# Four small filler tiles that move the split operands of the matmuls to the start of a 128-byte line of SBUF

## The chip, the cores and the metric

One core of a Trainium2 chip runs the whole program. The metric is the device time of one execution in microseconds (us). TensorE (PE in the profile) multiplies, ScalarE (ACT), VectorE (DVE) and GpSimd (POOL) do the rest, and SyncE (SP) issues the DMAs.

## The reference

The input is 256 tokens of 1024 features. It goes through two layers of a first block (here: layers A) and two of a second (layers B), all in float32. A layer is a mixer (projections, linear or gated recurrences, attention), a gated feed-forward network with 2816 hidden features, and a gate that adds a projected side input. The core of it:

```
u = rms_norm(h, g);  parts = split(u @ w_in);  ... mixers ...
h = h + (mixed @ w_out)                         # A: with a norm after it
g, u = split(rms_norm(h) @ w_ffn_in);  h = h + (silu(g) * u) @ w_ffn_out
h = h + gate(h @ w_ple_gate) * (p @ w_ple_proj)
```

A layer B has a second feed-forward network ahead of its mixer.

## The kernel before, in words

**Every product is three matmuls.** A float32 operand x is split into xh, its rounding to the type float32r that TensorE reads in one pass, and xl, what the rounding leaves. The product is xh·wh + xl·wh + xh·wl. The weights come as tiles of [128, 1024] float32 (512 KB): `weight` (lines 219 to 243) lets SP fetch one into `raw` (4 buffers), ScalarE writes `hi` (L241) and VectorE `lo` (L242), five buffers each. SP fetches ahead, as far as buffers are free, and ACT and DVE split ahead of TensorE.

**Two loops use them.** `gemm_fm` (lines 263 to 285) has the weights as the stationary operand, a block of 128×128 each, and lets 256 columns of the split input stream by (L279 to L281): 24 matmuls to a weight tile. `gemm_tm` (lines 287 to 317) has a block of the split input stationary and streams 512 columns of `hi` or `lo` (L306 to L308): 12 matmuls to a weight tile. In the trace, "acc<-xTh,hi" at L279 is a matmul that streams xTh against the stationary hi, and "acc<-hi,xTh" at L306 one that streams hi against the stationary xTh. TensorE loads the next stationary block while the matmul ahead of it streams.

**The split inputs** are the pairs xTh/xTl (normed input of every projection, pool `act`), hh/hl (hidden features of the network), oh/ol, yh/yl and mh/ml (inside the mixers), xrh/xrl (input of layer A's last gate, class `Raw`) and px (the side input).

**Where tiles lie.** A pool takes a stretch of bytes of each of the 128 partitions, and pools and tiles are laid one behind the other in the order in which the code makes them, each tile in a whole number of 32 bytes. The order is `const`, `wraw`, `whl`, `act`, `small` (lines 185 to 193), then `tmp` (temporaries), `hT` in layers B, and a pool of each mixer or network. The scheduler orders the instructions by priorities and a simulated timeline, and knows nothing of where a tile lies within a line.

The first pool, `const`, starts on a multiple of 128 bytes and holds ident (512 bytes), h (8192), expo (64) and ones (512): 9280 bytes, which is 72 lines of 128 and 64 over. So `raw`, `hi` and `lo` (4096 each) and xTh, xTl (8192 each) begin 64 bytes into a line. What a tile's first byte is past the start of a 128-byte line, called its phase here, is by the same addition:

| tiles | phase before | phase after |
|---|---|---|
| raw, hi, lo, xTh, xTl | 64 | 0 |
| hh, hl, xrh, xrl of layers A | 96 | 0 |
| hh, hl of layers B | 0 | 0 |
| oh, ol, mh, ml of layers A | 0 | 0 |
| oh, ol, yh, yl, mh, ml, left, right of layers B | 96 | 0 |
| px made in layers A / in layers B | 96 / 0 | 96 / 0 |
| ra, up (the matmuls "z", L821) | 0 | 0 |
| ident, h | 0 | 64 |
| temporaries t of layers A / layers B | 96 / 0 | 96 / 0 |

The slices that matmuls read start 512, 1024 or 2048 bytes apart, so that a slice has the phase of its tile. The third column is the same addition with the fillers of the change. [...]

Of the kernel before, what the change touches and what calls it, by code (L numbers as in the profile page):

```python
# [11 lines left out]
F32 = mybir.dt.float32  # L12
# [6 lines left out]
P = 128  # L19
# [19 lines left out]
HOLD_LAST = (1, 3)  # L39
HOLD_B = 4  # L40
LAG = 3


class Norm:
# [3 lines left out]
    def __init__(self, net, g, tag="xT"):  # L48
        self.net, self.g = net, g
        self.xs = net.pair(net.act, tag)  # L50
        self.r = [None, None]
        self.R = net.act.tile([P, S], F32, tag="R", name=net.name("R"), bufs=2)
        self.ssq = [net.small.tile([P, 2], F32, tag="nssq", name=net.name("nssq")) for _ in range(2)]
# [124 lines left out]
class Net:  # L178
    def __init__(self, ctx, tc, a, raw_bufs=4, w_bufs=5, acc_bufs=3):
        self.tc = tc  # L180
        self.nc = tc.nc
        self.a = a
        pool = lambda name, bufs, **kw: ctx.enter_context(tc.tile_pool(name=name, bufs=bufs, **kw))
        psum = bass.MemoryType.PSUM
        self.const = pool("const", 1)
        self.wraw = pool("wraw", raw_bufs)
        self.whl = pool("whl", w_bufs)
        self.act = pool("act", 1)
        self.small = pool("small", 4)
        self.ps = pool("ps", acc_bufs, space=psum)  # L190
        self.pt = pool("pt", 2, space=psum)
        self.pm = pool("pm", 2, space=psum)
        self.pg = pool("pg", 1, space=psum)
        self.n = 0


        self.hold = self.held = None
        self.fetched = []
        nc = self.nc
        self.ident = self.const.tile([P, P], F32, name="ident")  # L200
        self.h = self.const.tile([P, 2, D], F32, name="h")
        self.expo = self.const.tile([P, 16], F32, name="expo")
        nc.vector.memset(self.expo, -0.5)
        self.ones = self.const.tile([P, P], F32, name="ones")
        nc.vector.memset(self.ones, 1.0)

    def temporaries(self, ctx, bufs):
        self.tmp = ctx.enter_context(self.tc.tile_pool(name=self.name("tmp"), bufs=1))
        self.tmp_bufs = bufs
# [164 lines left out]
    def ffn(self, nrm, wi, wo, epi, pool, fm=False):  # L374
# [21 lines left out]
        else:  # L396
            self.gemm_tm((hh, hl), wo, epi, lag=LAG)

# [110 lines left out]
def layer_a(net, i, nrm, following):  # L509
    nc, a, tc = net.nc, net.a, net.tc  # L510
    with ExitStack() as mx:
        nrm, px = mixer_a(net, i, mx, nrm)
    with tc.tile_pool(name=net.name("ffn"), bufs=1) as fp:
        g_post = net.gain(a["g_ffn_post"][i])
        e = ple_proj(net, px, a["w_ple_proj"][i])
        raw = Raw(net, fp)
        net.ffn(nrm, a["w_ffn_in"][i], a["w_ffn_out"][i], net.post_norm(g_post, raw, fp, HOLD_FFN), fp)
        g_post = net.gain(a["g_ple_post"][i])
        nrm = following()
        px = ple_input(net, a["pT_2"][0]) if i + 1 == DEPTH else None  # L520

        def gated(tt, hf, acc):
            cs = slice(hf * 512, (hf + 1) * 512)
            t = net.t()
            nc.scalar.activation(t, acc, AF.Sigmoid)
            nc.vector.tensor_tensor(t, t, e[:, tt, cs], ALU.mult)
            return t

        net.gemm_tm(raw.xs, a["w_ple_gate"][i], net.post_norm(g_post, nrm, fp, HOLD_PLE if i + 1 < DEPTH else HOLD_LAST, gated), lag=LAG)
    return nrm, px  # L530


def ple_input(net, pT):
    with net.urgent(SPLIT_PRIO, 200):
        raw = net.t()
        net.nc.sync.dma_start(out=raw, in_=pT)
        px = (net.t((P, 2, S), F32R, "px"), net.t((P, 2, S), F32R, "px"))
        net.split_fm(raw, *px, 0)
    return px


def ple_proj(net, px, w):
    nc = net.nc
    e = net.t((P, 2, D), tag="e")
    net.gemm_tm(px, w, lambda tt, hf, acc: nc.scalar.copy(e[:, tt, hf * 512:(hf + 1) * 512], acc))
    return e
# [98 lines left out]
def mixer_a(net, i, cx, nrm):  # L645
# [40 lines left out]
    def rope_heads(tt, acc, nh, w, dst, h0):  # L686
        n = nh * P
        x = net.t()[:, :n]
        nc.scalar.activation(x, acc, AF.Copy, scale=r[tt])
        return lambda: rope_rest(tt, x, nh, w, dst, h0)  # L690
# [21 lines left out]

    net.gemm_tm(xs, a["w_aq"][i], lambda tt, hf, acc: rope_heads(tt, acc, 4, 0, q_t, hf * 4), lag=LAG if i else 0)
    if i == 0:
# [92 lines left out]
    px = ple_input(net, a["pT"][i])  # L807
    net.gemm_tm(ms, a["w_out"][i], net.post_norm(g_post, nrm, p1, HOLD_MIX, tags={"hg": "gg", "xg": "b1", "yg": "b0"}), lag=LAG)
    return nrm, px
# [84 lines left out]
def layer_b(net, i, nrm, px, hT, following):  # L894
# [12 lines left out]
    with ExitStack() as cx:  # L907
        ms = mixer_b(net, i, cx, after)
        px = ple_input(net, a["pT_2"][i])
        nrm = NormT(net, hT, col(2))  # L910
        net.gemm_fm(ms, a["w_o"][i], net.add_scaled(hT, 1.0, nrm.blocks), tail=True)
# [20 lines left out]
def mixer_b(net, i, cx, nrm):  # L932
    nc, a, tc = net.nc, net.a, net.tc
    p1 = cx.enter_context(tc.tile_pool(name=net.name("mx"), bufs=1))
    big = lambda tag, dt=F32: p1.tile([P, KB, S], dt, tag=tag, name=net.name(tag))
    fl = lambda t: t.rearrange("p a b -> p (a b)")
    xs, rs = nrm.xs, nrm.r
# [143 lines left out]
def _build(tc, a, out):  # L1081
    with ExitStack() as ctx:
        net = Net(ctx, tc, a)
        nc = tc.nc
        with ExitStack() as part:
            net.temporaries(part, T_BUFS_A)
            net.split = SPLIT_A
            nrm = lambda pool: first_norm(net, pool)
            nxt = [lambda: Norm(net, net.gain(a["g_mix_pre"][1])), lambda: Norm(net, net.gain(a["ffn1_norm_2"][0]))]
            for i in range(DEPTH):  # L1090
                nrm, px = layer_a(net, i, nrm, nxt[i])

        hp = ctx.enter_context(tc.tile_pool(name="hT", bufs=1))
        net.hp = hp
        net.temporaries(ctx, T_BUFS_B)
        net.split = SPLIT_B
        hT = hp.tile([P, KB, S], F32, name="hT")
        for tt in range(2):
            for hf in range(2):
                ps = net.pt.tile([P, 4, P], F32, tag="pt", name=net.name("pt"))  # L1100
                for j in range(4):
                    kb = hf * 4 + j
                    nc.tensor.transpose(ps[:, j], net.h[:, tt, kb * P:(kb + 1) * P], net.ident)
                nc.scalar.copy(hT[:, hf * 4:hf * 4 + 4, tt * P:(tt + 1) * P], ps)
        gc = hp.tile([P, 16], F32, name="gc")
        nc.sync.dma_start(out=gc, in_=a["gains_last"])
        nxt = [lambda: NormT(net, hT, gc[:, 0:8]), lambda: NormT(net, hT, gc[:, 8:16], out)]
        for i in range(DEPTH):
            nrm, px = layer_b(net, i, nrm, px, hT, nxt[i])
# [140 lines left out]
```

## Time and profile before

| | us |
|---|---|
| median of 3 runs | 2347.22 (2344.7 to 2348.76) |
| the profiled execution | 2343.83 |
| its span, first to last instruction | 2342.1 |
| TensorE busy in the span | 2292.5 |
| VectorE busy | 1602.7 |
| ScalarE busy | 1333.8 |
| mean share of the 16 DMA engines | 56% |

A matmul's busy time in the profile runs from its start to a modelled end, some 280 ns for 256 columns, and consecutive ones overlap. What a stream of matmuls costs is the distance between their starts. It is read from the first and the last start of a run and the count between: x instructions of one line, each followed by one of the two other lines of its loop, are 3(x-1) distances.

### The profile page before, as it was taken

The page shows a single profiled execution, that of the slowest core. Times are in us where ns is not written, and L with a number is a line of the kernel's source. Part 1 is how long each engine was busy: PE and PEld are TensorE (multiplying, and loading weights), DVE is VectorE, ACT ScalarE, POOL GpSimd, SP SyncE. Part 2 cuts the span into 40 slices and gives each one's busy share as a digit, 9 for nine tenths or more (in the row PEclk, how much of TensorE's full clock was granted, in tenths as well). Part 3 has the DMA queues.
Part 4 walks back from the last instruction along what each step waited for, and adds up shares of the span by engine and source line. Part 5 has one row for each costly group of instructions (what it writes and reads, how often), then busy time and mean ns, then how long its engine had stood idle before and what let it go on. Part 6 is the DMA issues. An engine that isn't in the chain of part 4 may idle for free.

```text
span 2342.1 us, 42188 instructions
## 1 busy us (share of the span) xinstructions
PE 2292.5 (98%) x16892; PEld 2176.4 (93%) x16892; DVE 1602.7 (68%) x2133; ACT 1333.8 (57%) x2105; POOL 441.0 (19%) x443
## 2 busy tenths in 40 slices
PE   8999999998999999999999999999999999999997
PEld 6899899878899998799999899999999998999997
DVE  7876766487867765665586867665755677766555
ACT  6874554467864644554456765444644557755444
POOL 5222111054302110211001302110111103012101
PEclk9999999999999999999999999999999999999999
DMA  7445566544455665546656555556556665456563
GB/s 253 145 153 162 186 196 182 180 167 146 146 162 176 203 184 183 174 163 182 190 182 189 161 152 183 184 186 197 172 181 188 188 188 168 149 169 190 181 190 99
DMA packets 117102, 411.53 MB, mean 176 GB/s; under 512 B 14114, under 2 KB 16546, under 8 KB 116906
## 3 DMA queue, kind: packets, MB, share of 16 engines
q1 hardware_dynamic: 116906, 408.84, 55.9%
q8 instruction: 133, 2.18, 0.4%
q14 instruction: 63, 0.52, 0.1%
HBM read 407.74 MB, written 1.05 MB: 175 GB/s over the span
## 4 chain that ended last, share of the span: by engine, by line
PE 89%; DVE 4%; POOL 3%; issue 2%; ACT 1%; DMA 1%; SPq 0%; DVEq 0%; POOLq 0%; ACTq 0%
PE acc L280 22%; PE acc L279 22%; PE acc L281 22%; PE acc L306 5%; PE acc L307 5%; PE acc L308 5%; DVE lo L242 1%; POOL t L703 1%; PE sc L572 1%; PE po L583 1%; PE gs L880 1%; ACT hi L241 1%; PE sc L596 0%; POOL hg L72 0%; DMA gq<-g_q_norm 0%
## 5 line engine op out<-in xcount | busy, mean ns | idle before, releaser
L242 DVE TENSOR_TENSOR lo<-raw,hi 128x512 fp32r<-128x512 f32 (+1 forms) x1062 | 985.5, 954 | 435.8 <-ACT hi L241 430.8
L241 ACT ACTIVATE hi<-raw 128x512 fp32r<-128x512 f32 (+1 forms) x1062 | 824.2, 808 | 764.5 <-PE acc L280 399.1
L279 PE MATMUL acc<-xTh,hi 128*128 128x256 f32 x3296 | 936.3, 284 | 8.8 <-ACT t L1049 7.2
L280 PE MATMUL acc<-xTl,hi 128*128 128x256 f32 x3296 | 938.8, 285 | 0.7 <-DVE xTl L127 0.5
L281 PE MATMUL acc<-xTh,lo 128*128 128x256 f32 x3296 | 936.5, 284 | 0.0
L279 PEld LDWEIGHTS acc<-xTh,hi 128*128 128x128 f32 x3296 | 634.4, 193 | 10.9 <-ACT t L1049 7.6
L280 PEld LDWEIGHTS acc<-xTl,hi 128*128 128x128 f32 x3296 | 634.6, 193 | 2.6 <-DVE xTl L127 1.5
L281 PEld LDWEIGHTS acc<-xTh,lo 128*128 128x128 f32 x3296 | 634.5, 193 | 0.4
L387 POOL TENSOR_TENSOR t<-t,R 128x512 f32<-128x512 f32 x66 | 105.8, 1603 | 624.6 <-ACT t L385 624.6
L279 PE MATMUL acc<-hh,hi 128*128 128x256 f32 x704 | 194.3, 276 | 0.0
L280 PE MATMUL acc<-hl,hi 128*128 128x256 f32 x704 | 194.3, 276 | 0.0
L281 PE MATMUL acc<-hh,lo 128*128 128x256 f32 x704 | 194.3, 276 | 0.0
L306 PE MATMUL acc<-hi,xTh 128*128 128x512 f32 x416 | 163.5, 398 | 6.5 <-ACT hi L241 6.5
L307 PE MATMUL acc<-lo,xTh 128*128 128x512 f32 x416 | 165.2, 397 | 1.4 <-DVE lo L242 1.3
L308 PE MATMUL acc<-hi,xTl 128*128 128x512 f32 x416 | 163.9, 395 | 0.1
L279 PEld LDWEIGHTS acc<-hh,hi 128*128 128x128 f32 x704 | 132.2, 188 | 0.0
L280 PEld LDWEIGHTS acc<-hl,hi 128*128 128x128 f32 x704 | 132.2, 188 | 0.0
L281 PEld LDWEIGHTS acc<-hh,lo 128*128 128x128 f32 x704 | 132.2, 188 | 0.0
L306 PEld LDWEIGHTS acc<-hi,xTh 128*128 128x128 f32 x416 | 78.7, 190 | 22.0 <-ACT hi L241 6.5
L307 PEld LDWEIGHTS acc<-lo,xTh 128*128 128x128 f32 x416 | 78.9, 190 | 17.9 <-DVE lo L242 2.7
L308 PEld LDWEIGHTS acc<-hi,xTl 128*128 128x128 f32 x416 | 78.7, 189 | 16.7 <-DVE xTl L342 0.8
L370 DVE TENSOR_TENSOR t<-acc,R 128x512 f32<-128x512 f32 (+1 forms) x84 | 56.9, 677 | 47.3 <-PE acc L281 46.3
(321 smaller groups left out, 3235.7 us busy)
## 6 DMA issues: line engine op xcount, KB each, us to landing
raw<-ffn_w_in SPq DMA_DIRECT2D x176, 512.0 KB, 3.7
raw<-w_ffn_in SPq DMA_DIRECT2D x88, 512.0 KB, 3.8
raw<-ffn_w_out SPq DMA_DIRECT2D x88, 512.0 KB, 3.6
raw<-w_ffn_out SPq DMA_DIRECT2D x44, 512.0 KB, 4.0
raw<-w_gate SPq DMA_DIRECT2D x32, 512.0 KB, 3.8
raw<-w_gab SPq DMA_DIRECT2D x32, 512.0 KB, 3.6
raw<-w_gqk SPq DMA_DIRECT2D x16, 512.0 KB, 3.7
raw<-w_gv SPq DMA_DIRECT2D x16, 512.0 KB, 3.4
```

What stands on the lines that cost most here:

```text
L241: nc.scalar.activation(hi[:, cs], raw[:, cs], AF.Copy)
L242: nc.vector.tensor_tensor(lo[:, cs], raw[:, cs], hi.bitcast(F32)[:, cs], ALU.subtract)
L279: nc.tensor.matmul(o, lhsT=hi[:, cs], rhs=xh[:, kb], start=kb == 0, stop=False)
L280: nc.tensor.matmul(o, lhsT=hi[:, cs], rhs=xl[:, kb], start=False, stop=False)
L281: nc.tensor.matmul(o, lhsT=lo[:, cs], rhs=xh[:, kb], start=False, stop=kb == nkb - 1)
L306: nc.tensor.matmul(o, lhsT=xh[:, kb, ts], rhs=hi[:, cs], start=kb == 0, stop=False)
L307: nc.tensor.matmul(o, lhsT=xh[:, kb, ts], rhs=lo[:, cs], start=False, stop=False)
L308: nc.tensor.matmul(o, lhsT=xl[:, kb, ts], rhs=hi[:, cs], start=False, stop=kb == 2 * n - 1)
L370: self.nc.vector.tensor_tensor(v(out), v(acc), r, ALU.mult)
L387: nc.gpsimd.tensor_tensor(tb, tb, nrm.R.unsqueeze(1).to_broadcast([P, 2, S]), ALU.mult)
L572: nc.tensor.matmul(sc[:, j], lhsT=q_t[:, hp * 2 + j, tt * P:(tt + 1) * P], rhs=k_t[:, hp // 2], start=True, stop=True)
L583: nc.tensor.matmul(out[:, j], lhsT=v(jt, hp // 2), rhs=p_t[:, jt], start=jt == 0, stop=jt == 1)
```

## The change

`phase` makes a tile that nothing reads or writes; it only takes bytes. One of 64 bytes goes to the head of `const`, one of 64 bytes to the head of `small`, one of 32 bytes to the head of the network's pool of layers A, and one of 32 bytes to the head of the mixer's pool of layers B. No instruction is added, removed or moved.

```
--- before.py
+++ after.py
@@ -39,6 +39,9 @@
 HOLD_LAST = (1, 3)
 HOLD_B = 4
 LAG = 3
+
+X_PHASE = 64
+POOL_PHASE = 32
 
 
 class Norm:
@@ -192,6 +195,8 @@
         self.pm = pool("pm", 2, space=psum)
         self.pg = pool("pg", 1, space=psum)
         self.n = 0
+        self.phase(self.const, X_PHASE)
+        self.phase(self.small, X_PHASE)
 
 
         self.hold = self.held = None
@@ -203,6 +208,10 @@
         nc.vector.memset(self.expo, -0.5)
         self.ones = self.const.tile([P, P], F32, name="ones")
         nc.vector.memset(self.ones, 1.0)
+
+    def phase(self, pool, n):
+
+        pool.tile([P, n // 4], F32, tag="phase", name=self.name("phase"), bufs=1)
 
     def temporaries(self, ctx, bufs):
         self.tmp = ctx.enter_context(self.tc.tile_pool(name=self.name("tmp"), bufs=1))
@@ -511,6 +520,7 @@
     with ExitStack() as mx:
         nrm, px = mixer_a(net, i, mx, nrm)
     with tc.tile_pool(name=net.name("ffn"), bufs=1) as fp:
+        net.phase(fp, POOL_PHASE)
         g_post = net.gain(a["g_ffn_post"][i])
         e = ple_proj(net, px, a["w_ple_proj"][i])
         raw = Raw(net, fp)
@@ -932,6 +942,7 @@
 def mixer_b(net, i, cx, nrm):
     nc, a, tc = net.nc, net.a, net.tc
     p1 = cx.enter_context(tc.tile_pool(name=net.name("mx"), bufs=1))
+    net.phase(p1, POOL_PHASE)
     big = lambda tag, dt=F32: p1.tile([P, KB, S], dt, tag=tag, name=net.name(tag))
     fl = lambda t: t.rearrange("p a b -> p (a b)")
     xs, rs = nrm.xs, nrm.r
```

## Rows read from the trace of the kernel before

**Rows 1.** The page: the span, TensorE's busy time, and the chain that ended last.

```profile
span 2342.1 us, 42188 instructions
...
PE 2292.5 (98%) x16892; PEld 2176.4 (93%) x16892; DVE 1602.7 (68%) x2133; ACT 1333.8 (57%) x2105; POOL 441.0 (19%) x443
...
PE 89%; DVE 4%; POOL 3%; issue 2%; ACT 1%; DMA 1%; SPq 0%; DVEq 0%; POOLq 0%; ACTq 0%
PE acc L280 22%; PE acc L279 22%; PE acc L281 22%; PE acc L306 5%; PE acc L307 5%; PE acc L308 5%; DVE lo L242 1%; POOL t L703 1%; PE sc L572 1%; PE po L583 1%; PE gs L880 1%; ACT hi L241 1%; PE sc L596 0%; POOL hg L72 0%; DMA gq<-g_q_norm 0%
...
```

**Rows 2.** Busy time by engine in four stretches, with clock and DMA share.

```profile
...
280.40:406.80 126.40, 126.40 (x1055) 126.40 (x1055) 79.70 (x126) 65.56 (x116) 14.87 (x11) 1.00 0.62 192
406.90:468.20 61.30, 61.30 (x264) 49.31 (x264) 29.48 (x46) 25.56 (x47) 1.20 (x4) 1.00 0.56 180
...
1459.70:1580.00 120.30, 120.30 (x1005) 120.30 (x1004) 72.54 (x74) 56.60 (x66) 19.00 (x11) 1.00 0.60 188
1580.10:1639.80 59.70, 59.70 (x529) 59.70 (x529) 35.77 (x36) 28.69 (x34) 4.44 (x4) 1.00 0.63 195
...
```

**Rows 3.** Matmuls on xTh, a network of layer B: durations, first and last start.

```profile
...
L279 PE MATMUL acc<-xTh,hi x334: 283/283/283, 1459.8 to 1579.7; 128*128 128x256 f32 x167
...
```

**Rows 4.** Matmuls on hh, the next 60 us of that network.

```profile
...
L279 PE MATMUL acc<-hh,hi x176: 276/276/286, 1580.0 to 1639.6; 128*128 128x256 f32 x176
...
```

**Rows 5.** Matmuls on oh in layer A's mixer.

```profile
...
L281 PE MATMUL acc<-oh,lo x50: 276/276/279, 208.5 to 225.2; 128*128 128x256 f32 x50
...
```

**Rows 6.** Matmuls on oh in layer B's mixer.

```profile
...
L281 PE MATMUL acc<-oh,lo x61: 277/280/282, 1405.9 to 1427.1; 128*128 128x256 f32 x61
...
```

**Rows 7.** 512-column matmuls with xTh stationary, layer B.

```profile
...
L306 PE MATMUL acc<-hi,xTh x32: 389/389/396, 1215.3 to 1236.4; 128*128 128x512 f32 x32
...
```

**Rows 8.** 512-column matmuls with mh stationary, layer A.

```profile
...
L306 PE MATMUL acc<-hi,mh x32: 388/388/394, 248.3 to 269.6; 128*128 128x512 f32 x32
...
```

**Rows 9.** 512-column matmuls with hh stationary, layer A.

```profile
...
L306 PE MATMUL acc<-hi,hh x88: 392/394/399, 406.8 to 467.7; 128*128 128x512 f32 x88
...
```

**Rows 10.** TensorE in order of time around a z pair: start us, us, instruction.

```profile
...
68.12 0.28 PE L281 MATMUL acc<-xTh,lo 128*128 128x256 f32 x1
68.24 0.40 PE L821 MATMUL z<-ra,up 98*128 98x256 f32 x2
68.48 0.28 PE L279 MATMUL acc<-xTh,hi 128*128 128x256 f32 x1
...
69.55 0.28 PE L279 MATMUL acc<-xTh,hi 128*128 128x256 f32 x1
...
```

**Rows 11.** Groups over the whole span: line, operation, xcount | busy us, mean ns.

```profile
...
L279 PE MATMUL acc<-xTh,hi 128*128 128x256 f32 x3296 | 936.3, 284 | 8.8 <-ACT t L1049 7.2 <-ACT t L689 1.5
...
L279 PE MATMUL acc<-hh,hi 128*128 128x256 f32 x704 | 194.3, 276 | 0.0
...
L306 PE MATMUL acc<-hi,xTh 128*128 128x512 f32 x416 | 163.5, 398 | 6.5 <-ACT hi L241 6.5
...
L279 PE MATMUL acc<-oh,hi 128*128 128x256 f32 x256 | 70.9, 279 | 0.0
...
L306 PE MATMUL acc<-hi,hh 128*128 128x512 f32 x176 | 66.5, 396 | 0.0
...
L279 PE MATMUL acc<-yh,hi 128*128 128x256 f32 x128 | 36.0, 282 | 0.0
...
L279 PE MATMUL acc<-mh,hi 128*128 128x256 f32 x128 | 35.1, 280 | 0.0
...
L306 PE MATMUL acc<-hi,xrh 128*128 128x512 f32 x64 | 25.1, 398 | 0.0
...
L306 PE MATMUL acc<-hi,mh 128*128 128x512 f32 x64 | 24.0, 390 | 0.0
...
L339 PE MATMUL pt<-ident,hg 128*128 128x128 f32 x64 | 11.1, 315 | 6.6 <-DVE hg L82 5.0 <-DVE xTl L342 1.6
...
L1021 PE MATMUL rg<-yh,hi 128*128 128x256 f32 x32 | 9.0, 282 | 0.0
...
```

**Rows 12.** ScalarE's groups, 280.4 to 406.8 us: the split of hh.

```profile
...
L355 ACT ACTIVATE hh<-t 128x512 fp32r<-128x512 f32 x10 | 6.2, 619 | 1.0 <-DVE t L390 1.0
...
```

**Rows 13.** ScalarE's groups, 1459.7 to 1580 us: the same split.

```profile
...
L355 ACT ACTIVATE hh<-t 128x512 fp32r<-128x512 f32 x10 | 6.1, 613 | 0.0
...
```

More of the change, by code (lines that the diff above doesn't have):

```diff
@@ L41 @@
 LAG = 3
+X_PHASE = 64
+POOL_PHASE = 32
 class Norm:
@@ L194, in __init__ @@
         self.n = 0
+        self.phase(self.const, X_PHASE)
+        self.phase(self.small, X_PHASE)
         self.hold = self.held = None
@@ L205, in __init__, with phase @@
         nc.vector.memset(self.ones, 1.0)
+    def phase(self, pool, n):
+        pool.tile([P, n // 4], F32, tag="phase", name=self.name("phase"), bufs=1)
     def temporaries(self, ctx, bufs):
@@ L513, in layer_a @@
     with tc.tile_pool(name=net.name("ffn"), bufs=1) as fp:
+        net.phase(fp, POOL_PHASE)
         g_post = net.gain(a["g_ffn_post"][i])
@@ L934, in mixer_b @@
     p1 = cx.enter_context(tc.tile_pool(name=net.name("mx"), bufs=1))
+    net.phase(p1, POOL_PHASE)
     big = lambda tag, dt=F32: p1.tile([P, KB, S], dt, tag=tag, name=net.name(tag))
```

## The prediction

> **What bounds the kernel.** I read the page first. TensorE is busy 2292.5 of 2342.1 us, and the chain that ended last lies on it for 89%, almost all of that in the six lines of the two loops [rows 1]. So 49.6 us of the span are idle time of TensorE, and the rest is a stream of matmuls: what counts is the distance between their starts. The view of busy time in stretches says next that inside the loops nothing else binds. [...]
>
> [...] In a network of layer B the 334 matmuls of L279 on xTh start from 1459.8 to 1579.7 us: 119.9 us over 3 x 333 distances, 120.0 ns each [rows 3]. The next product of the same network, the same loop and lines, with hh streamed: 59.6 us over 3 x 175, 113.5 ns [rows 4]. Both have hi and lo (phase 64) stationary; xTh has phase 64 and hh phase 0. That the length of the sum over blocks (8 or 22) makes the difference is ruled out by oh, which has 8 as xTh has: in layer A, at phase 0, 16.7 us over 3 x 49, 113.6 ns [rows 5]; in layer B, at phase 96, 21.2 us over 3 x 60, 117.8 ns [rows 6]. So a 256-column matmul costs 113.5 ns from phase 0, about 117.8 from 96 and 120.0 from 64. The times read to 0.1 us leave 0.2 to 0.7 ns on the last digits. [...]
>
> With 512 columns the streamed hi and lo always have phase 64. With xTh stationary (64): 21.1 us over 3 x 31, 226.9 ns [rows 7]; with mh stationary (0): 21.3 us over 93, 229.0 ns [rows 8]; with hh stationary (96): 60.9 us over 3 x 87, 233.3 ns [rows 9]. [...]
>
> **The change, part by part.** No instruction comes or goes, and none is moved past a queue; the fillers are never written, so no wait is added. All the change does is in the phases.
>
> *256 columns, xTh and xTl, 64 to 0.* L279, L280 and L281 have 3296 each [rows 11]: 9888 x (120.0 - 113.5) = 64.3 us less.
>
> *256 columns from 96 to 0.* In layers B yh (3 x 128), oh (half of 3 x 256), mh (3 x 128) and the gates' yh at L1021 and the two lines below it (3 x 32) [rows 11]: 1248 x (117.8 - 113.5) = 5.4 us.
>
> *512 columns.* No row has hi and lo at phase 0. [...] xTh stationary, 3 x 416: 1248 x 6.5 = 8.1 us. hh and xrh stationary, 3 x (176 + 64) = 720 [rows 11]: 233.3 to 220.4, 9.3 us. mh stationary, 192: 229.0 to 220.4, 1.7 us. Together 19.1; at the upper price 5.0 (nothing for xTh, 4.6 and 0.4 for the others), at the lower 34.4.
>
> *Streams that were at 0 already.* hh and layer B's px (2112 + 72) and half of oh (384) change only their stationary side, hi and lo, from 64 to 0. One row shows both sides at 0: a pair of z matmuls inside a run on xTh. From the first z at 68.24 to the eleventh matmul behind it at 69.55 us go 1.31 us, where eleven distances of 120.0 make 1.32 [rows 10]. [...] I take 113.5 for both sides at 0. [...]
>
> *Transposes.* ident, streamed in 360 transposes such as L339's [rows 11], goes from 0 to 64. Bounds: nothing, or at most 6.5 ns each, 2.3 us. I take nothing: a float32 transpose is not one of the float32r streams that the rows above price, and its share is small either way.
>
> *ScalarE, VectorE, DMA.* Their operands move too. ScalarE's split of hh takes 619 ns with t and hh at 96 [rows 12] and 613 with both at 0 [rows 13]: 1%, and these engines have room [rows 2]. The transfers into raw land at phase 0 instead of 64; at 0.56 to 0.63 of the DMA engines a few per cent either way stay hidden. What hides them is a stream that gets 5.5% shorter; VectorE's 63.1% becomes 66.7%, DMA's 0.63 at most 0.67. That cover holds.
>
> *What is late next.* 49.6 us of idle time stay, and a part of them grows, where products cover a chain of other engines (attention, scans, norms) and end sooner now. I take a tenth of them, 5 us.
>
> Sum: 64.3 + 5.4 + 19.1 = 88.8, less 5, is 83.8 us. From the profiled execution's own 2343.8 that leaves 2260. That execution ran 3.4 us (0.15%) below the median of 2347.2, inside what the three runs spread; I leave the forecast at **2260**. About 0.2%, 4.7 us, is what a measurement of this kernel can tell from no change.
>
> **The rivals.**
>
> *Slower: it is the two sides starting at the same place of a line that costs.* While one matmul streams, the next block is loaded. Today the stationary hi and lo are at 64, so that 64, 96 and 0 on the streamed side are 0, 32 and 64 bytes apart from it, and the 256-column rows fit that order as well as mine. After the change all pairs are 0 apart. Then xTh stays at 120.0, the 2568 streams from hh, oh and px rise by 6.5 (16.7 us), the 1248 from 117.8 to 120.0 (2.7), and of the 512s hh and xrh fall to 226.9 (4.6) and mh by 2.1 (0.4): 14.4 us more, 2361 with the median. It decides wherever hh with hi shows 120. Against it stand the z pair [rows 10], and the 512s, where equal phases are the cheapest [rows 7 to 9]. Chance 0.06.
>
> *Nothing happens:* a tile that nobody uses gets no bytes, or the phase of the streamed side is not what the rows show. 2347. Against it stands that the groups of rows 3 to 6 differ by phase with the same code and lines. Chance 0.03. [...]
>
> [...] Chance 0.06. [...]
>
> *Half is given back.* Only the networks' long runs keep the gain: 6 x 1056 of the xTh matmuls (41.2 us) and 528 with hh stationary (6.8); in the mixers the chains of other engines set the pace, and there 40.8 us turn into waits. 2296. For it: the idle time sits at the mixers' ends. Against it: TensorE is idle for 49.6 us only, so that the products, not the chains, fill the mixers today. Chance 0.08.
>
> **How the numbers follow.** My case has 0.77. Its own range is 2240 to 2285: the gain of the 512s can be 15.3 us larger or 14.1 smaller, the idle time some 5 to 8 us off, and the median stood 3.4 above. The range reaches on to the half gain, 2240 to 2296, and leaves out the slower case, no change and the bigger gain, 0.15, with a little of my own. Faster by over 0.2%: 0.77 + 0.06 + 0.08 = 0.91; within: 0.03; slower: 0.06.
>
> **What would show it.** In the changed kernel the distance between xTh's starts should be 113.5 ns (duration 276 and not 283), hh's unchanged at 113.5, layer B's oh at 113.5, the 512s all the same near 220 whatever is stationary, clock still 1.00, idle time near 55 us. 120 for hh makes the first rival true, below 112 the third; idle time of 90 us or more the fourth; 512s at 227 would cost my sum 14 us.

## The result, and the profile after

The changed kernel takes **2361.56 us** (median of 4 runs, 2361.22 to 2362.57) where the kernel before takes 2346.13 on the same chip: ratio 1.0064, 95% interval 1.0052 to 1.0076. It is 15.4 us slower; the forecast was 2260. The page of the changed kernel (gemm_fm's lines are now L288 to L290, gemm_tm's L315 to L317):

```profile
span 2360.8 us, 42188 instructions
...
PE 2309.8 (98%) x16892; PEld 2197.3 (93%) x16892; DVE 1605.0 (68%) x2133; ACT 1334.8 (57%) x2105; POOL 439.0 (19%) x443
...
PE 89%; DVE 5%; POOL 3%; issue 1%; DMA 1%; ACT 1%; SPq 0%; DVEq 0%; POOLq 0%; ACTq 0%
...
L288 PE MATMUL acc<-xTh,hi 128*128 128x256 f32 x3296 | 937.1, 285 | 9.2 <-ACT t L1060 7.3
...
L288 PE MATMUL acc<-hh,hi 128*128 128x256 f32 x704 | 199.2, 283 | 0.0
...
L315 PE MATMUL acc<-hi,xTh 128*128 128x512 f32 x416 | 163.6, 399 | 6.5 <-ACT hi L250 6.5
...
```

TensorE is still the bound and idle for 51.0 us of the span, 49.6 before [rows 1]; its busy time grew by 17.3 us. The last columns of the three groups (busy us, mean ns of one) tell where: hh went from 276 to 283 ns, while xTh and the 512s moved by 1 ns [rows 11]. The views of single tiles (count, duration min/median/max, first and last start) give the distances, as in rows 3 to 9:

```profile
...
L288 PE MATMUL acc<-xTh,hi x334: 281/283/283, 1465.0 to 1584.9; 128*128 128x256 f32 x167
...
L288 PE MATMUL acc<-hh,hi x166: 283/283/283, 1585.2 to 1644.6; 128*128 128x256 f32 x166
...
L288 PE MATMUL acc<-oh,hi x60: 283/283/287, 1410.1 to 1431.4; 128*128 128x256 f32 x60
...
L315 PE MATMUL acc<-hi,xTh x32: 389/389/396, 1219.2 to 1240.3; 128*128 128x512 f32 x32
...
L315 PE MATMUL acc<-hi,hh x88: 389/389/396, 409.0 to 468.2; 128*128 128x512 f32 x88
...
```

xTh: 119.9 us over 999 distances, 120.0 ns, as in [rows 3]. hh: 59.4 over 495, **120.0 instead of 113.5** [rows 4]. oh in layer B: 21.3 over 177, 120.3 instead of 117.8 [rows 6]. With 512 columns xTh stationary stays at 21.1 / 93 = 226.9 [rows 7], and hh stationary falls from 233.3 to 59.2 / 261 = 226.8 [rows 9]. So every 256-column stream whose two sides are both at 0 now costs what only xTh cost, and every such 512-column one what only xTh's cost: the first rival's picture. Only the px of layers A (24 streams of 256 columns, 48 of 512) are not at 0 with hi and lo. Over the whole trace, distances over 145 ns (stalls) set aside, the 13,720 streams of 256 columns with both sides at 0 (the 16 z matmuls among them) have a mean of 119.9 ns; before, the 9888 of xTh had 119.9, 2568 had 113.4 and 1272 had 117.7.

### The profile page after: what moved, and what is told of

Read it like the earlier page. It is cut to its first block, busy times and chain, and to the rows that moved or that the text cites. A ratio compares the mean times of both kernels' runs of the same rounds, so it can differ in the third digit from the quotient of the medians.

```text
span 2360.8 us, 42188 instructions
## 1 busy us (share of the span) xinstructions
PE 2309.8 (98%) x16892; PEld 2197.3 (93%) x16892; DVE 1605.0 (68%) x2133; ACT 1334.8 (57%) x2105; POOL 439.0 (19%) x443
## 4 chain that ended last, share of the span: by engine, by line
PE 89%; DVE 5%; POOL 3%; issue 1%; DMA 1%; ACT 1%; SPq 0%; DVEq 0%; POOLq 0%; ACTq 0%
PE acc L289 22%; PE acc L290 22%; PE acc L288 22%; PE acc L315 5%; PE acc L316 5%; PE acc L317 5%; DVE lo L251 2%; POOL t L713 1%; PE sc L582 1%; PE po L593 1%; PE gs L890 1%; ACT hi L250 0%; PE sc L606 0%; POOL tab L689 0%; DMA gq<-g_q_norm 0%
## 5 line engine op out<-in xcount | busy, mean ns | idle before, releaser
L288 PE MATMUL acc<-xTh,hi 128*128 128x256 f32 x3296 | 937.1, 285 | 9.2 <-ACT t L1060 7.3
L290 PE MATMUL acc<-xTh,lo 128*128 128x256 f32 x3296 | 937.1, 285 | 0.0
L288 PEld LDWEIGHTS acc<-xTh,hi 128*128 128x128 f32 x3296 | 635.2, 193 | 11.3 <-ACT t L1060 7.7
L290 PEld LDWEIGHTS acc<-xTh,lo 128*128 128x128 f32 x3296 | 635.3, 193 | 0.4
L290 PE MATMUL acc<-hh,lo 128*128 128x256 f32 x704 | 199.2, 283 | 0.0
L288 PE MATMUL acc<-hh,hi 128*128 128x256 f32 x704 | 199.2, 283 | 0.0
L289 PE MATMUL acc<-hl,hi 128*128 128x256 f32 x704 | 199.2, 283 | 0.0
L315 PE MATMUL acc<-hi,xTh 128*128 128x512 f32 x416 | 163.6, 399 | 6.5 <-ACT hi L250 6.5
L317 PE MATMUL acc<-hi,xTl 128*128 128x512 f32 x416 | 164.0, 395 | 0.1
L288 PEld LDWEIGHTS acc<-hh,hi 128*128 128x128 f32 x704 | 135.2, 192 | 0.0
L290 PEld LDWEIGHTS acc<-hh,lo 128*128 128x128 f32 x704 | 135.2, 192 | 0.0
L315 PEld LDWEIGHTS acc<-hi,xTh 128*128 128x128 f32 x416 | 78.7, 190 | 22.5 <-ACT hi L250 7.0
L317 PEld LDWEIGHTS acc<-hi,xTl 128*128 128x128 f32 x416 | 78.8, 189 | 16.7 <-DVE xTl L351 0.8
```

The source lines that it names most:

```text
L288: nc.tensor.matmul(o, lhsT=hi[:, cs], rhs=xh[:, kb], start=kb == 0, stop=False)
L289: nc.tensor.matmul(o, lhsT=hi[:, cs], rhs=xl[:, kb], start=False, stop=False)
L290: nc.tensor.matmul(o, lhsT=lo[:, cs], rhs=xh[:, kb], start=False, stop=kb == nkb - 1)
L315: nc.tensor.matmul(o, lhsT=xh[:, kb, ts], rhs=hi[:, cs], start=kb == 0, stop=False)
L317: nc.tensor.matmul(o, lhsT=xl[:, kb, ts], rhs=hi[:, cs], start=False, stop=kb == 2 * n - 1)
```

## The experiments

What was left to find out is what sets the distance: the streamed operand's own place, or how far it lies from the operand that is loaded meanwhile, and modulo what. In small programs (first, fifth and seventh run) nothing but matmuls runs and none of the reference is computed, so their total times mean nothing. A "distance" is the first byte of the split input (xs in the small programs) less that of the weights (ws), modulo 256, whichever of the two streams.

**A first map of distances.** `fm` streams 256 columns of xs against 128 of ws, as gemm_fm does, 192 matmuls to a name; the tiles' first bytes are moved by slices.

```
+        def fm(name, dx, dw):
...
+            def body(acc, k, first, last):
+                j = k // 3
+                x = (j % 8) * 256 + (2048 if k % 3 == 1 else 0) + dx[k % 2]
+                w = (j % 8) * 128 + (1024 if k % 3 == 2 else 0) + dw[k % 2]
+                nc.tensor.matmul(acc[:, :256], lhsT=ws[:, w:w + 128], rhs=xs[:, x:x + 256], start=first, stop=last)
```

> The kernel leaves the whole computation out and only runs streams of 192 float32r matmuls with nothing else beside them; its time says nothing, the distance between starts does. Series f streams 256 columns of a tile x against blocks of a tile w that begins on a line; x is 0, 16, 32, 48, 64, 80, 96, 112, 128, 192, 256 and 384 bytes on (fa to fl). Series t streams 512 columns of w against blocks of x at 0 to 112, 128 and 192 bytes (ta to tj). Theory of the distance (what costs is how far the streamed operand and the block that is loaded meanwhile lie apart within a line): fa, fi, fk and fl 120.0 ns, fe and fj 113.5, fc and fg about 117.8, the rest between; ta and ti 226.9, te and tj 229.0, tc 233.3. gboth (both sides at 32) 120.0, gfar (x at 0, w at 64) 113.5. Rival of the stationary side (a block loaded from the start of a line costs the stream 6.5 ns, whatever streams): all of fa to fl 120.0, gfar 113.5. Rival of the streamed side, the prediction's own: fa 113.5, fe 120.0, gfar 113.5. Two runs tell which load counts: in gown the even matmuls have both sides at 0 and the odd ones both at 64, so that a matmul and its own block are 0 apart and a matmul and the next one's block 64; in gnext it is the other way round. If the block loaded while a matmul streams is the next one's, gown takes 113.5 and gnext 120.0; if a matmul's own block counts, gown 120.0 and gnext 113.5.

The tile rows of five names, with 0, 64, 128, 256 and 384 bytes between slice starts:

```profile
...
L46 PE MATMUL fa<-xs,ws x192: 279/281/582, 14.6 to 39.1; 128*128 128x256 f32 x192
...
L46 PE MATMUL fe<-xs,ws x192: 276/276/284, 107.7 to 129.3; 128*128 128x256 f32 x192
...
L46 PE MATMUL fi<-xs,ws x192: 280/283/283, 197.6 to 220.5; 128*128 128x256 f32 x192
...
L46 PE MATMUL fk<-xs,ws x192: 279/281/285, 243.2 to 265.9; 128*128 128x256 f32 x192
...
L46 PE MATMUL fl<-xs,ws x192: 277/283/283, 266.0 to 288.9; 128*128 128x256 f32 x192
...
```

xs itself began 128 bytes past a multiple of 256, which the expectation did not count, so these are true distances of 128, 192, 0, 128 and 0 modulo 256. From the 41st matmul on they are 118.7, 113.3, 120.0, 118.7 and 120.0 ns. The pattern comes back after 256 bytes and not after the 128 in which I had counted phases. gboth, which moves both tiles 32 bytes on from fa and so stays 128 apart, takes 118.6, as fa and fk do; gfar, 64 apart with both tiles elsewhere than in fj, takes 117.8 as fj does: so far the distance counts, and not the place. gown and gnext took 116.7 and 118.4 and, at true distances of 128, 64 and 192 instead of the intended 0 and 64, could not say which load counts. With 512 columns true distances 0 and 240 were the cheapest, 226.7, against up to 233.3.

**The streamed side on its line, the weights not.** Against the changed kernel the filler moves from `const` to `act`: raw, hi and lo stay where they were before, every split input is where the change puts it.

```
-        self.phase(self.const, X_PHASE)
+        self.phase(self.act, X_PHASE)
```

> The changed kernel with the 64-byte filler at the head of the pool act and not of const: raw, hi and lo stay at 64 as before, every split input (but the px of layers A) is at 0, so that streamed and loaded operands lie 64 bytes apart in all of the 256-column products. Theory of the distance: all 256-column streams at 113.5 ns (64.3 + 5.4 us less than before), the 512-column ones all at 229.0 (xTh 1248 x 2.1 = 2.6 us more, hh and xrh 720 x 4.3 = 3.1 less), together about 70 us less than before: 2276 us, ratio 0.970, faster than both kernels. Rival that the slowdown came from elsewhere (the transfers, ScalarE, VectorE, ident off its line, the order of the work): the 256-column streams may go to 113.5, but the time stays 10 us or more above that sum.

Measured: 2342.79 us, ratio to before 0.9987 (0.9978 to 0.9996); the 2276 missed by 67. The tile rows of xTh (a network of layer A), hh (layer B) and hh stationary:

```profile
...
L288 PE MATMUL acc<-xTh,hi x351: 279/279/280, 282.1 to 405.7; 128*128 128x256 f32 x176
...
L288 PE MATMUL acc<-hh,hi x172: 279/279/279, 1577.0 to 1637.4; 128*128 128x256 f32 x172
...
L315 PE MATMUL acc<-hi,hh x88: 394/394/397, 406.1 to 467.0; 128*128 128x512 f32 x88
...
```

123.6 us over 1050 distances, 60.4 over 513: 117.7 ns for both, and 60.9 / 261 = 233.3 with 512 columns, where 229.0 was expected. **xTh lies at the same place as in the changed kernel and costs 117.7 instead of 120.0, because the weights lie elsewhere.** So the streamed side's own phase does not set its time. The distance here is 64 modulo 256; the 113.4 that hh had before stood at 192, which modulo 128 is the same 64. That is why 2276 failed.

**The change without the two pools' fillers.** Against the changed kernel:

```
-        net.phase(fp, POOL_PHASE)
-    net.phase(p1, POOL_PHASE)
```

> The change without the two 32-byte fillers: weights and xTh at 0, the tiles that were at 96 stay there. Theory of the distance: xTh stays at 120.0, hh of layers B, oh of layers A and px go from 113.5 to 120.0 (16.7 us more), the tiles at 96 stay at 117.8 and 233.3 with 32 bytes between the sides as before, mh of layers A gains 0.4: 16.3 us more than before, about 2362 us. Rival of the stationary side: the tiles at 96 go to 120.0 as well, 2.7 us more, and xTh as above. Rival of the streamed side: xTh at 113.5 and 64 us less.

Measured: 2362.78 us, ratio 1.0073 (1.0059 to 1.0087), a hit. The rows of hh and mh in layer B:

```profile
...
L288 PE MATMUL acc<-hh,hi x162: 283/283/283, 1586.8 to 1644.8; 128*128 128x256 f32 x162
...
L288 PE MATMUL acc<-mh,hi x64: 277/281/285, 1433.6 to 1456.0; 128*128 128x256 f32 x64
...
```

hh, at distance 0, takes 58.0 / 483 = 120.1 ns; mh, 224 from the weights, 22.4 / 189 = 118.5, against 117.7, the mean of the 1272 streams at distance 160 before. The pools' fillers thus have no part in the loss: it comes from the other two, which take hi and lo and layer B's hh to the same place.

**The two pools' fillers alone.** The weights and xTh stay 0 apart as before; everything else but the px of layers A comes to 192.

```
-        self.phase(self.const, X_PHASE)
-        self.phase(self.small, X_PHASE)
```

> The two 32-byte fillers alone: weights and xTh stay at 64, and the tiles that were at 96 go to 0, 64 bytes apart from hi and lo. Theory of the distance: xTh stays at 120.0, the 1248 matmuls of layers B that were at 117.8 go to 113.5 (5.4 us less), hh and xrh of layers A as blocks go from 233.3 to 229.0 (3.1 less): 8.5 us less than before, about 2338, ratio 0.996. The rivals of the streamed and of the stationary side say the same of the 256-column streams; all of them fail if these stay at 117.8.

Measured: 2342.83 us, ratio 0.9987 (0.9978 to 0.9996), 5 us short of the expected 2338. The rows of oh in layer A, oh in layer B and hh in layer B, all at distance 192:

```profile
...
L286 PE MATMUL acc<-oh,hi x49: 276/276/277, 209.9 to 226.3; 128*128 128x256 f32 x49
...
L286 PE MATMUL acc<-oh,hi x60: 281/281/281, 1409.3 to 1430.2; 128*128 128x256 f32 x60
...
L286 PE MATMUL acc<-hh,hi x175: 276/276/286, 1583.6 to 1642.7; 128*128 128x256 f32 x175
...
```

16.4 / 144 = 113.9 for the first, with a median duration of 276. The second, 20.9 / 177 = 118.1, has 281 throughout; the third, 59.1 / 522 = 113.2, again 276. The same distance has two values.

**The map with both tiles at a multiple of 256, and streams after an interruption.**

Against the first small program:

```
-PAD = 160
+PAD = 128
...
+        pool.tile([P, 32], F32, name="fill")
         rawx = pool.tile([P, X + PAD], F32, name="rawx")
...
+        fm("fm", (48, 48), (0, 0))
...
+        gap(1)
+        fm("farb", (48, 48), (0, 0))
```

> Streams of 192 float32r matmuls again, the computation left out, with both tiles now at a multiple of 256 bytes, so that distances are known in 256. fa to fp: 256 columns, x 0 to 240 bytes on in steps of 16; ta to tp: 512 columns, the same. Theory that the distance counts within 256 bytes: fa 120.0, fe (64) 117.8, fi (128) 118.7, fm (192) 113.4; ta 226.7, ti 232.4, tm 228.9, te 233.3. Theory of 128: fe and fm equal, fa and fi equal. gown and gnext step the tiles in cycles of four: in gown a matmul's own block is 0 and the next one's 192 bytes away from what it streams, in gnext the own block 192 and the next one's 0. If the next one's load counts: gown 113.4, gnext 120.0; if the own: the reverse; if the load after the next: neither. fara to farf (192 bytes apart) and neara to nearf (64) come each behind other work on TensorE: one, two or eight float32 matmuls, four short ones, or a wait for VectorE. Theory of two states: the distance of an interrupted stream does not follow from the bytes alone, and some of these twelve settle at 113.4 and some at 117.8; if the bytes alone decide, all far are 113.4 and all near 117.8.

Rows of the distances 0, 112, 128 and 192:

```profile
...
L47 PE MATMUL fa<-xs,ws x192: 277/283/579, 14.3 to 39.6; 128*128 128x256 f32 x192
...
L47 PE MATMUL fh<-xs,ws x192: 275/275/275, 175.5 to 197.1; 128*128 128x256 f32 x192
...
L47 PE MATMUL fi<-xs,ws x192: 274/281/287, 197.2 to 219.9; 128*128 128x256 f32 x192
...
L47 PE MATMUL fm<-xs,ws x192: 276/276/284, 288.2 to 309.9; 128*128 128x256 f32 x192
...
```

From the 41st matmul on: 120.0, 113.3, 118.6, 113.3 ns (the first name has a slow start, and at 128 durations run from 274 to 287). After other matmuls had interrupted, 192 gave 113.3 four times and 117.8 twice, 64 gave 113.3 twice and 117.8 four times; 64 had 113.3 in its own uninterrupted run. So both have two values. The 512s stood at 226.7 at 0 and within 16 bytes of it, and at 228.9 to 234.3 from 32 to 224. Two names of mixed distances fit no simple rule: 118.3 where a matmul's own block is 0 away and the next one's 192, 117.5 the other way round, while distance 0 gives 120.0 and 192 gives 113.3 or 117.8. Neither the own nor the next block alone sets the time, and which one counts stays open.

**All streamed tiles 192 from the weights** (but the px of layers A, 24 streams). The kernel of the second run with another size of one filler:

```
-        self.phase(self.act, X_PHASE)
+        self.phase(self.act, 192)
```

> The changed kernel with a filler of 192 bytes at the head of act in place of the 64 bytes at the head of const: raw, hi and lo at 192 within 256 bytes as before, all split inputs (but the px of layers A) at 128, the distance at which hh ran in the kernel before. Theory of 256: xTh 113.4 (64.3 us less than before), the 1248 at 96 113.4 (5.4 less), 512 columns all at 228.9 (2.6 more, 3.1 less): about 2276 us, faster than both. Theory of two states: part of the streams settle at 117.8 and the gain is between 25 and 70 us: 2276 to 2321. Theory of 128 (e2 at another absolute place): 2343, as e2.

Measured: **2326.33 us**, ratio 0.9913 (0.9896 to 0.993): faster than both kernels, 5 us outside the range that two values gave. The rows of xTh in the network of the first layer A, of the second, and of hh in a layer B:

```profile
...
L288 PE MATMUL acc<-xTh,hi x351: 276/276/278, 278.8 to 397.8; 128*128 128x256 f32 x176
...
L288 PE MATMUL acc<-xTh,hi x351: 281/281/281, 764.1 to 887.7; 128*128 128x256 f32 x176
...
L288 PE MATMUL acc<-hh,hi x168: 281/281/281, 1563.8 to 1622.8; 128*128 128x256 f32 x168
...
```

119.0 / 1050 = 113.3 ns, then 123.6 / 1050 = 117.7 for the same lines and addresses modulo 256; hh 59.0 / 501 = 117.8. The value holds from one interruption to the next, and the timeline ahead of the two networks shows the same instructions in the same order. What picks the value I could not see. The mean over all 13,704 streams, stalls aside, is 116.6.

**Six starts to each distance.** The small program again, with six kinds of interruption (`gap`) ahead of six streams of 96 at each distance of 16 bytes:

```
+        gap(2)
+        fm("fhc", (28, 28), (0, 0))
```

> Streams of 96 float32r matmuls, the computation left out. Every distance from 0 to 240 bytes in steps of 16 (fa to fp, 256 columns) is run six times, each time behind one of the six pieces of other work of e5 (second letter a to f); five distances also with 512 columns (ta 0, tb 16, th 112, tm 192, tp 240). se, sh, si and sm run 64, 112, 128 and 192 bytes behind a stream at 0 with nothing between. Theory of two states: fe and fm take 113.3 or 117.8 depending on what stood ahead, and 64 and 192 bytes are then the same case seen from two starts; sm, which has no interruption ahead of it, 113.3 as hh in the kernel before; fa 120.0 in all six. A distance whose six runs all stay under 115 would be a place where the whole kernel gains 6.5 ns on every 256-column matmul; by the rival that the bytes alone decide, each distance has one value in all six runs, and e5's low runs at 64 bytes were something else.

Rows of 112 (first and third start), 192 (first and third), and of 512 columns at 0 and at 112:

```profile
...
L47 PE MATMUL fha<-xs,ws x96: 275/275/470, 555.9 to 566.9; 128*128 128x256 f32 x96
...
L47 PE MATMUL fhc<-xs,ws x96: 275/275/367, 579.6 to 590.6; 128*128 128x256 f32 x96
...
L47 PE MATMUL fma<-xs,ws x96: 276/276/469, 938.4 to 949.3; 128*128 128x256 f32 x96
...
L47 PE MATMUL fmc<-xs,ws x96: 280/281/365, 962.0 to 973.3; 128*128 128x256 f32 x96
...
L75 PE MATMUL taa<-ws,xs x96: 387/389/580, 1244.2 to 1266.0; 128*128 128x512 f32 x96
...
L75 PE MATMUL tha<-ws,xs x96: 389/394/584, 1526.6 to 1548.9; 128*128 128x512 f32 x96
...
```

The duration tells the value: 275 is 113.3 ns, 276 the fast and 281 the slow value of 192 (113.3 and 117.8). From the 26th matmul on **112 had 113.33 or 113.34 in all six starts**, 192 had 113.3 three times and 117.8 three times, 64 had 117.8 six times, 0 and 96 had 120.0 (0 once 120.1, with a stall in it); no other distance was ever below 116.6. Two values are not special to 64 and 192: 16 and 144 had 118.7 or 116.7, 80 had 120.0 or 118.4, 160 had 118.7 or 117.3. With 512 columns 0 gave 226.7 six times and 112 gave 233.3 six times, while 16 gave 226.7 twice and 233.3 four times, 192 gave 228.9 five times and 233.3 once, 240 gave 226.7 four times and 228.4 twice. Directly behind a stream at distance 0, with no interruption, 192 gave 113.3: that is how hh stood behind xTh in the kernel before, in the networks of layers B.

**Distance 112 in the whole kernel.** Streamed tiles get a 16-byte slice offset inside a padded tile, and fillers for the rest; tiles of layers A that are only stationary (hh, xrh) come to 0. oh and mh of layers A and px stay where they are.

```
+    def off(self, pool, tag, n, a, pad):
+        t = pool.tile([P, n + pad], F32R, tag=tag, name=self.name(tag))
+        return t[:, 4:4 + n].rearrange("p (a b) -> p a b", a=a)
...
+        self.fill(self.act, 96)
+        self.fill(self.small, 128)
...
+        if pool is self.act:
+            xh = self.off(pool, tag + "h", KB * S, KB, 8)
+            self.fill(pool, 224, "fillb")
+            return xh, self.off(pool, tag + "l", KB * S, KB, 8)
...
+        if fm:
+            self.fill(pool, 160)
+            hh, hl = (self.off(pool, "h" + c, NHB * S, NHB, 64) for c in "hl")
...
+        net.fill(fp, 96)
...
+    net.fill(p1, 192)
```

> The streamed tiles of the 256-column products (the normed input everywhere; hh, oh, yh, mh and their low halves in layers B) begin 112 bytes behind hi and lo, modulo 256, and the stationary-only tiles hh and xrh of layers A begin 0 apart from hi and lo. My theory, the distance modulo 256 with 112 as a distance that has only the fast value (all six starts of the run before): every 256-column stream at 113.3 to 113.4 ns, 9888 x 6.6 = 65.3 us and 1248 x 4.4 = 5.5 us less; 512 columns with the normed input stationary rise from 226.9 to 233.3, 8.0 us more; with hh and xrh of layers A they fall to 226.9, 4.6 us less; 5 us more of stalls: 2284 us, ratio 0.973. Rival, 112 has two values in the whole kernel as 192 had: a mean near 115.6, 2314 us, ratio 0.986. Rival, the small program does not carry over at this distance: nothing of the 65 us, 2340 to 2350.

Measured: **2288.03 us** (2285.6 to 2289.45), ratio 0.9748 (0.9731 to 0.9764): 58.5 us faster than before, 4 from the expected 2284 and far from the rivals' 2314 and 2340. The page:

```profile
span 2286.4 us, 42188 instructions
...
PE 2232.6 (98%) x16892; PEld 2111.8 (92%) x16892; DVE 1600.5 (70%) x2133; ACT 1334.6 (58%) x2105; POOL 444.0 (19%) x443
...
L290 PE MATMUL acc<-xTh,hi 128*128 128x256 f32 x3296 | 911.8, 277 | 10.0 <-ACT t L1078 8.0
...
L290 PE MATMUL acc<-hh,hi 128*128 128x256 f32 x704 | 193.6, 275 | 0.0
...
L317 PE MATMUL acc<-hi,xTh 128*128 128x512 f32 x416 | 165.6, 404 | 6.0 <-ACT hi L252 6.0
...
```

Busy time of TensorE is 59.9 us below [rows 1], idle time 53.8 us. The tile rows of xTh (layer A, layer B), hh (layer B), and the 512s with hh and xTh stationary:

```profile
...
L290 PE MATMUL acc<-xTh,hi x351: 275/275/282, 280.0 to 399.1; 128*128 128x256 f32 x176
...
L290 PE MATMUL acc<-xTh,hi x334: 275/275/283, 1430.0 to 1543.2; 128*128 128x256 f32 x167
...
L290 PE MATMUL acc<-hh,hi x172: 275/275/275, 1544.9 to 1603.1; 128*128 128x256 f32 x172
...
L317 PE MATMUL acc<-hi,hh x87: 389/389/389, 400.1 to 458.6; 128*128 128x512 f32 x87
...
L317 PE MATMUL acc<-hi,xTh x30: 394/394/394, 1190.0 to 1210.3; 128*128 128x512 f32 x30
...
```

119.1 / 1050 = 113.4, 113.2 / 999 = 113.3, 58.2 / 513 = 113.5 ns; 58.5 / 258 = 226.7 and 20.3 / 87 = 233.3. In these rows every distance stands where it was put. Over the whole trace, stalls aside, the streams at 112 have a mean of 113.7, and of the gain the 256-column streams give about 64 us, the 512s take about 1 (xTh dearer, hh and xrh cheaper), and stalls grow by about 7, where 5 was expected: 56 us less together, where the two spans differ by 55.7. The networks stay bound by TensorE (columns as in [rows 2]):

```profile
...
280.40:400.00 119.60, 119.60 (x1055) 119.52 (x1054) 80.33 (x126) 65.46 (x116) 14.92 (x11) 1.00 0.67 203
1430.00:1540.00 110.00, 110.00 (x973) 110.00 (x972) 70.33 (x72) 54.99 (x63) 17.21 (x10) 1.00 0.66 196
...
```

VectorE is busy for 67.2% of the first stretch (80.33 of 119.60) and the DMA engines for 0.67, where the forecast had 66.7% and 0.67 for such a gain.

## Why the prediction was wrong

**What bounds the kernel** was read rightly: the time is the distance between matmuls' starts, and each run's time follows from those distances by the counts of [rows 11], but for some us of stalls. ScalarE and VectorE stayed hidden as said: 1334.8 and 1605.0 us busy after, 1333.8 and 1602.7 before. The transposes I took as nothing; no run took them apart.

**The step that failed is "256 columns, xTh and xTl, 64 to 0": the reading of rows 3 to 6 as the streamed side's own phase.** The rows fitted two rules, its phase and its distance from the stationary side, as the first rival itself said. They could not part the two, since hi and lo had one place in all of them. Rows 7 to 9 could have warned me: there hi and lo stream from one place throughout, and the time still went from 226.9 to 233.3 with the place of the stationary tile. The second run parts them: xTh at the same place, the weights moved, 117.7 instead of 120.0. So the 64.3 us were 0, and the 5.4 of "from 96 to 0" became 2.8 us more (1248 x 2.2).

**The row that decided between them was misread: "Streams that were at 0 already".** I took the z pair [rows 10] as both sides at 0 costing less than 120. After the change everything around that pair is at 0 as well. TensorE in order of time:

```profile
...
69.00 0.28 PE L290 MATMUL acc<-xTh,lo 128*128 128x256 f32 x1
69.12 0.40 PE L831 MATMUL z<-ra,up 98*128 98x256 f32 x2
69.36 0.28 PE L288 MATMUL acc<-xTh,hi 128*128 128x256 f32 x1
...
70.44 0.28 PE L288 MATMUL acc<-xTh,hi 128*128 128x256 f32 x1
...
```

From the first z at 69.12 to the eleventh matmul behind it at 70.44 us are 1.32 us: eleven times 120.0, where before it was 1.31. Both sides at 0 give nothing back. The row of before had said so too: from the first z at 68.24 to the first xTh behind the pair at 68.48 are 0.24 us, two distances of 120, and the 10 ns that 1.31 lacks of 1.32 were missing behind that, between 68.48 and 69.55, where xTh streams alone [rows 10]. The starts in ns give the eleven distances as 121, 119, then 122, 116, 119, 116, 119, 119, 121, 116 and 118, 1306 together; from the twelfth on they are 120 again. So the pair, whose tiles lay 64 bytes from those around it, unsettled the streams behind it for nine distances, as the three other pairs inside runs on xTh did; now that all lie alike, none leaves such a mark. Why the nine came out shorter no run shows. I had put down to the pair what came after it. With 120.0 for both sides at 0 the 2568 streams of hh, oh and px cost 16.9 us more.

**"512 columns"**: 220.4 was my guess by analogy, and no run shows it, nor the lower price behind the 34.4 and the 15.3: the small programs had 226.7 to 234.3 ns, and in the changed kernel the upper price, 226.9, was what came: 4.6 us less for hh and xrh, 0.4 for mh, none for xTh. The first rival's sum, with the measured distances 16.9 + 2.8 - 4.6 - 0.4 = 14.7 us (14.4 as it was put), stands against 15.4 measured. It had a chance of 0.06 for the most part on the strength of a 10 ns difference in a row rounded to 10 ns; what else was held against it, that equal phases are the cheapest for the 512s, is true (226.7 ns at distance 0), and holds for them alone.

**"What is late next"**, 5 us, did not come into play (idle time 51.0 against 49.6). Where the streams did become shorter, in the last run, idle time rose by 4.2 us, near the 5 that I took, and nothing like the fourth rival's 40 us came.

## What to carry to other kernels

With float32r streams of 256 columns and a new block for each, choose where the streamed tile starts relative to the stationary one, modulo 256 bytes, not where it lies by itself: 112 cost 113.3 ns, 0 cost 120.0, and with 512 columns 0 was best, at 226.7; a slice offset of 16 bytes in a padded tile reaches what fillers of 32 cannot. When rows fit two rules, look for the one row in which only one of the two factors differs, and read its neighbours too, before a chance of 0.06 is written down. A small program that steps the factor through its whole period costs one run and would have shown here that such streams gain nothing from the start of a 128-byte line: 120.0 ns at distance 0, 118.6 at 128.

## What the hardware did that was not expected

- The distance counts modulo 256 bytes (fa and fk of the first map, 256 bytes apart, both cost 118.7 ns, fi and fl both 120.0), and not in its size: 0 and 96 cost 120.0 ns, 112 beside them 113.3, 240 costs 117.1. I have no rule for the order.
- Distances of 64 and 192 have two values, 113.3 and 117.8 ns, and 16, 80, 144 and 160 have two that lie 1.3 to 2.0 ns apart; a stream keeps the one it starts with until other matmuls interrupt it (1053 in a row at either in the sixth run). Of the 16 distances 112 alone had 113.3 each time. What picks the value stays open; so do which of the following blocks counts, steps finer than 16 bytes, and hi and lo at different places for the two loops.
- 512 columns want the opposite: 226.7 ns at distance 0, mostly 228.9 at 192, 233.3 at 64 and at 112. The runs show that the distance between the two operands sets the time, not where inside the chip.
- No steady stream of 256 columns went below 113.3 ns at any of the 16 distances, and so none below the 112 that "What would show it" set for the third rival.
